# A down projection by seven products: the sums made early, in an order of their own, in place of operands that are done with

## The chip, the cores and the metric

The kernel runs on one core of a Trainium2 chip. The engines of that core are TensorE (PE in the profile, its weight loads PEld), VectorE (DVE), ScalarE (ACT), GpSimd (POOL) and SyncE (SP, which here only issues transfers). The metric is the device time of one execution in microseconds (us), lower is better. Before the change it is 1359.8 us, the median of three runs (1359.43 to 1360.07).

## The reference, cut to what matters

One layer: conditioning, two kinds of attention, an output projection, and a gated MLP with a short convolution. Only the last product of the MLP is touched here:

```python
h = modulate(rmsnorm(x, g_mlp_norm[l]), sh_m, sc_m)
u = causal_dwconv(jnp.dot(h, w_up[l]), conv_w[l], conv_b[l])
gate, val = jnp.split(u, 2, axis=-1)
x = x + g_m[:, None, :] * jnp.dot(jax.nn.silu(gate) * val, w_down[l])
```

`silu(gate) * val` is 1024 x 2816, called g below; `w_down` is 2816 x 1024. All is float32.

## The kernel before, in words

**The product.** The MLP's first half runs a loop over the 22 blocks of 128 columns of g (`for j in range(NF)`); it writes each block, transposed, to the buffer `g_d` in HBM (`store_g`). The down projection then reads g and `w_down` back. It multiplies them as 2 x 2 blocks with seven products in place of eight (a Strassen-Winograd scheme). A is g in four blocks (A11, A12, A21, A22), B is `w_down` in four (B11 to B22), and the kernel's seven products are, in the order in which it runs them (`order`, L1719):

| product | left operand | right operand |
|---|---|---|
| 1 | A11 | B11 |
| 2 | A12 | B21 |
| 7 | S3 = A11 - A21 | T3 = B22 - B12 |
| 6 | S2 = A22 - S3 | T2 = T3 + B11 |
| 5 | S1 = A21 + A22 | T1 = B12 - B11 |
| 3 | S4 = A12 - S2 | B22 |
| 4 | A22 | T4 = T2 - B21 |

**The steps.** Each product is accumulated over NK2 = 11 blocks k of 128 inner rows. `seq` lists the 77 pairs (product, k); one pair is called a step below, numbered 0 to 76: product 1 has steps 0 to 10, product 2 steps 11 to 21, product 7 steps 22 to 32, product 6 steps 33 to 43, product 5 steps 44 to 54, product 3 steps 55 to 65, product 4 steps 66 to 76. Both operands of a step are 128 x 512. For accuracy each operand is split into a rounded high part and the rest (`halves`, L1762 on: the high part by ACT, L81; the rest by DVE, L87), and a step is 4 output tiles times 3 matmuls (`mm3`, L1858 to L1860): high by high, high by low, low by high. The split operands lie in buffers `dpa` and `dpb`, five steps deep in all. Where an operand is a sum made on POOL, `halves` first copies it into PSUM by ACT (the "staged" flag, L1770, tiles `sga` and `sgb`), and DVE reads that copy.

**The sums.** `operands(i)` (L1741 on) makes a step's sums on POOL (L1744) at the point where that step's halves are written, that is, LEAD = 4 steps before TensorE's loop reaches it. The S3 sum is the one exception: it is made one product early, in product 2. Four buffers per k are kept for long: `held_a[k]` (A11, then S3, then S2), `held_b[k]` (B11) and `tsum[k]` (T3, then T2). S1, T1, S4 and T4 are written over one of the operands loaded for them.

**The loads.** Apart from the blocks of product 1, which go straight to their held buffers, every operand is loaded (`get`, `fetch`, L1704, issued by SP) into a slot of the tag "ws", of which there are ten of 128 x 512. `load_down(i)` loads what step i needs, `advance` keeps AHEAD = 4 steps beyond the one whose halves are written. Counted over all seven products there are 13 loads into slots for each k: 3 in product 2 (B21, A12, A21), 2 in product 7, 1 in product 6, 3 in product 5, 2 in product 3, 2 in product 4. There are 8 sums for each k.

**The ends of the products.** `finish_tile` empties the accumulated banks: product 2 stores its output after a multiplication by the gate row on DVE and an addition of the residual on POOL (L1834); product 6 adds on DVE and on POOL (L1829); product 5 has three DVE and three POOL operations per tile (L1837 to L1843), product 3 two on DVE and one on POOL (L1845 to L1847), product 4 two on DVE.

**What sets the order.** The program is written in the order of the loops. A scheduler that runs while the program is built then orders each engine's instructions by that order as priority and by simulated readiness, and gives tiles their slots; semaphores are added by it. On the chip each engine, and SP's queue of transfers, runs in the fixed order that results.

Of the kernel before, what the change touches and what calls it, by code (L numbers as in the profile page):

```python
# [12 lines left out]
F32 = mybir.dt.float32  # L13
# [8 lines left out]
MUL, ADD, SUB, MIN, MAX = ALU.mult, ALU.add, ALU.subtract, ALU.min, ALU.max  # L22

P = 128
# [5 lines left out]
NF = FF // P  # L30
# [17 lines left out]
PRE = 2  # L48
HI_ON, HL_BUFS = "pa", 3
VSCALE = 2.0 ** 14  # L50
UP_W = (3.2, 2.0)


# [15 lines left out]
def layer_kernel(ctx, tc, I, out):  # L69
    nc = tc.nc  # L70
    pe, act, dve, pool, sp = nc.tensor, nc.scalar, nc.vector, nc.gpsimd, nc.sync
# [412 lines left out]
    for d in range(ND):  # L484
# [25 lines left out]
        for t in range(NT):  # L510
            h, j = divmod(t, 4)
# [14 lines left out]
    def pow2_scale(nm, ssw, b2, n, fac):  # L526
# [11 lines left out]
        dve.tensor_scalar(t[:, 2, 1:2].bitcast(I32), t[:, 2, 1:2].bitcast(I32), 0x7F800000, None, op0=ALU.bitwise_and)  # L538
        dve.tensor_scalar(ab[:, 0:1], t[:, 2, 0:1], VSCALE, None, op0=MUL)
        dve.tensor_scalar(ab[:, 1:2], t[:, 2, 1:2], 1.0 / VSCALE, None, op0=MUL)  # L540
        return ab[:, 0:1], ab[:, 1:2]
# [298 lines left out]
    def f_up(gr):  # L840
        for c in f_up_steps(gr):
            yield c * UP_W[gr]

# [167 lines left out]
    def f_pre():  # L1011
        pages = [pgtile([P, 2, 2, 512], F16, f"wpp{i}") for i in range(2)]
        count = 0
        for j in range(PRE):
# [14 lines left out]
            for x in range(4):  # L1029
                pe.matmul(pt[:, 0:1], ones[:], t[:, x:x + 1], start=(x == 0), stop=(x == 3))  # L1030
            dve.tensor_scalar(t[:, 4:5], pt[:, 0:1], 1.0 / VSCALE ** 2, 1e-20, op0=MUL, op1=ADD)
            pool.tensor_tensor(t[:, 5:6], t[:, 4:5], phalf[:], op=ALU.pow)
# [310 lines left out]
    W_IN, W_M, W_UP, W_O = 21.0e3, 36.4e3, 13.0e3, 41.5e3  # L1343
    W_A = 5 * W_IN + W_M + W_UP * UP_W[0]
    W_B = W_UP * UP_W[1] + W_O
    C_CA, C_M = 6.95e3, 8.05e3
# [135 lines left out]
    def scale_ff(j, pt):  # L1482
# [5 lines left out]
        for i in range(2):  # L1488
            pe.matmul(pt[:, 0:1], ones[:], t[:, i:i + 1], start=(i == 0), stop=(i == 1))
        dve.tensor_scalar(t[:, 2:3], pt[:, 0:1], 1.0 / VSCALE ** 2, 1e-20, op0=MUL, op1=ADD)  # L1490
        pool.tensor_tensor(t[:, 3:4], t[:, 2:3], phalf[:], op=ALU.pow)
# [86 lines left out]
    def bank(tag, name, n=1):  # L1578
        return ps3.tile([P, n * 512], F32, name=name, tag=tag, bufs=1)
# [12 lines left out]
    def ff_first(j, w, held=None):  # L1592
        c = fc[j] = mt("c", [P, 7, 512], f"c{j}")
        p1 = bank("p1", f"p1_{j}")
        product(p1[:], w[0], "b11")
        act.activation(c[:, 0], p1[:], AF.Copy)
        if held:
            ff_second(j, w[1], held)
# [6 lines left out]
    def ff_tile(j):  # L1605
        held = j < 2
        w = gens.pop(j) if held else ff_w(j)
        if not held:
            ff_first(j, [next(w)])
        c = fc.pop(j)  # L1610
        p5, p6 = (bank(n, f"{n}_{j}") for n in ("p5", "p6"))
        p27, p34 = bank("p27", f"p27_{j}", 2), bank("p34", f"p34_{j}", 2)
        if not held:
            product(p27[:, :512], next(w), "b21")
        product(p27[:, 512:], next(w), "t3")
        product(p6[:], next(w), "t2")
        dve.tensor_tensor(c[:, 6], c[:, 0], p6[:], op=ADD)
        if held:
            dve.tensor_tensor(c[:, 0], c[:, 0], c[:, 5], op=ADD)
            dve.tensor_tensor(c[:, 5], c[:, 6], p27[:, 512:], op=ADD)  # L1620
        else:
            dve.tensor_tensor(c[:, 0::5][:, 0:2], c[:, 0::6][:, 0:2], p27[:].rearrange("p (a b) -> p a b", a=2), op=ADD)
        product(p5[:], next(w), "t1")
        dve.tensor_tensor(c[:, 3:5], c[:, 5:7], p5[:].unsqueeze(1).to_broadcast([P, 2, 512]), op=ADD)
        product(p34[:, 512:], next(w), "t4")
        product(p34[:, :512], next(w), "b22")
        raws.pop(j, None)
        dve.tensor_tensor(c[:, 1:3], c[:, 4:6], p34[:].rearrange("p (a b) -> p a b", a=2), op=ADD)  # L1628
        cg = c[:, 0:2].rearrange("p a b -> p (a b)")
        cv = c[:, 2:4].rearrange("p a b -> p (a b)")  # L1630
        ug, uv = conv(cg, j, 0), conv(cv, j, 1)
        act.activation(ug[:], ug[:], AF.Silu)
        dve.tensor_tensor(ug[:], ug[:], uv[:], op=MUL)
        gout.append((j, ug))
# [56 lines left out]
    NK2 = NF // 2  # L1691
    held_a, held_b, tsum = {}, {}, {}
    dpool = {}
# [20 lines left out]
    def drop(nm):  # L1714
        return mt("ws", [P, 512], nm)[:]

    plan = {1: ("A11", "B11"), 2: ("A12", "B21"), 7: ("S3", "T3"), 6: ("S2", "T2"), 5: ("S1", "T1"), 3: ("S4", "B22"),
            4: ("A22", "T4")}
    order = [1, 2, 7, 6, 5, 3, 4]  # L1719
    seq = [(p, k) for p in order for k in range(NK2)]  # L1720
    BL = {"A11": 0, "A12": 1, "A21": 2, "A22": 3, "B11": 0, "B12": 1, "B21": 2, "B22": 3}

    def get(nm, k, p):
        o = drop(f"{nm}_{p}_{k}")
        return fetch(o, (g_src if nm[0] == "A" else w_src)(BL[nm], k))

    loaded = {}

    def load_down(i):
        p, k = seq[i]  # L1730
        if p == 1:
            held_a[k], held_b[k] = hold("ha", k), hold("hb", k)
            fetch(held_b[k], w_src(0, k))
            fetch(held_a[k], g_src(0, k))
            loaded[i] = ()
        else:
            need_ = {2: ("B21", "A12", "A21"), 7: ("B22", "B12"), 6: ("A22",), 5: ("B12", "A21", "A22"), 3: ("B22", "A12"),
                     4: ("B21", "A22")}[p]
            loaded[i] = [get(nm, k, p) for nm in need_]

    def operands(i):  # L1741
        p, k = seq[i]
        x = loaded.pop(i)
        tt = lambda o, a, b, op: (pool.tensor_tensor(o, a, b, op=op), o)[1]  # L1744
        if p == 1:
            return (held_a[k], 0), (held_b[k], 0)
        if p == 2:
            tt(held_a[k], held_a[k], x[2], SUB)
            return (x[1], 0), (x[0], 0)
        if p == 7:  # L1750
            t = tsum[k] = dpool["r"].tile([P, 512], F32, name=f"tsum{k}", tag=f"tsum{k}")[:]
            return (held_a[k], 1), (tt(t, x[0], x[1], SUB), 1)
        if p == 6:
            return (tt(held_a[k], x[0], held_a[k], SUB), 1), (tt(tsum[k], tsum[k], held_b[k], ADD), 1)
        if p == 5:
            return (tt(x[1], x[1], x[2], ADD), 1), (tt(x[0], x[0], held_b[k], SUB), 1)
        if p == 3:
            return (tt(x[1], x[1], held_a[k], SUB), 1), (x[0], 0)
        return (x[1], 0), (tt(x[0], tsum[k], x[0], SUB), 1)

    def halves(i):
        p, k = seq[i]  # L1762
        pgs = []
        for nm, (src, staged) in zip("ab", operands(i)):
            pl, n = (dna, 4) if i % 5 < 2 else (dnb, 6)
            w = pl.tile([P, 2, 512], F32R, name=f"dp{nm}{p}_{k}", tag="dp", bufs=n)
            hi_of("a", w[:, 0], src)
            if staged:
                sg = ps4.tile([P, 512], F32, name=f"sg{nm}{p}_{k}", tag="sg", bufs=2)
                act.activation(sg[:], src, AF.Copy)  # L1770
                src = sg[:]
            lo_of("v", w[:, 1], src, w[:, 0])
            pgs.append(w)
        return pgs
# [3 lines left out]
    for j in range(NF):  # L1778
        if j + 3 < NF:
            load_ff(j + 3)  # L1780
        if j >= NF - 3:
            load_down(j - NF + 3)
        store_g()
        if j == NF - 1:
            ready_p += [halves(0), halves(1)]
        ff_tile(j)
        if j + 2 < NF:
            scale_ff(j + 2, bank("G", f"wss_ps{j + 2}"))
        if j >= 4:
            next(gate, None)  # L1790
# [68 lines left out]
        pe.matmul(b, g[:, 0, sl], w[:, 1], start=False, stop=False, **kw)  # L1859
        pe.matmul(b, g[:, 1, sl], w[:, 0], start=False, stop=end, **kw)  # L1860

    AHEAD = 4
    nl = [3]

    def advance(i):
        while nl[0] < min(len(seq), i + AHEAD):
            load_down(nl[0])
            nl[0] += 1

    for i, (p, k) in enumerate(seq):  # L1870
        if i == 4:
            store_g()
        while len(ready_p) + i < min(len(seq), i + LEAD):
            m = len(ready_p) + i
            advance(m)
            with tc.high_priority(offset=200) if m < 6 else nullcontext():
                ready_p.append(halves(m))
        if k == 0 and p != 2:
            for t in range(4):
                banks[t] = ps4.tile([P, 512], F32, name=f"q{p}{t}", tag="q", bufs=6)  # L1880
        tail = p == 4 and k >= NK2 - 3
        if tail and k > NK2 - 3:
            continue
        steps = ready_p[:3] if tail else ready_p[:1]
        if not tail:
            ready_p.pop(0)
        for t in range(4):
            for x, (g, w) in enumerate(steps):
                mm3(t, w, g, k == 0 and p != 2, k + x == NK2 - 1)
            if k + len(steps) == NK2:  # L1890
                finish_tile(p, t)
# [79 lines left out]
```

## Time and profile before

| | |
|---|---|
| median of three runs | 1359.8 us |
| the profiled execution's own time | 1360.98 us |
| its span, first to last instruction | 1359.2 us |
| mean granted TensorE clock | 0.969 |
| TensorE busy | 1263.4 us, 93% of the span |
| DVE, ACT, POOL busy | 75%, 64%, 56% |
| matmuls of the down projection | 924, from 1137.95 us to the end of the span |

A row of a group reads: line, engine, operation, output<-inputs by the program's names, shapes, count | busy us, mean ns of one | idle time of the engine just before them, and what ended it. In a row of the stages the count stands in brackets behind each engine's busy time, then come the granted clock, the mean busy share of the 16 transfer engines and their GB/s. Times of rows are us from the start of the span. Loads appear as `A<-g_d` and `B<-w_down` (slots) or `ha<-g_d` and `hb<-w_down` (held buffers); a sum appears with its output in place, as `ha<-ha,A` (S3), `tsum<-B,B` (T3), `ha<-A,ha` (S2), `tsum<-tsum,hb` (T2), `A<-A,A` (S1), `B<-B,hb` (T1), `A<-A,ha` (S4) and `B<-tsum,B` (T4).

### The profile page before, as it was taken

How to read it: one execution, taken by the hardware profiler on the slowest of the kernel's cores; microseconds unless marked ns; L12 is line 12 of the kernel's file. 1: busy time of each engine (PE TensorE's matmuls, PEld its weight loads, DVE VectorE, ACT ScalarE, POOL GpSimd, SP SyncE). 2: the span in 40 equal slices, each digit the busy share in tenths (PEclk: the TensorE clock that was granted, in tenths of full speed). 3: DMA queues.
4: the chain of work that ended last, by engine and by line, in shares of the span. 5: the costliest groups of instructions: out<-in, count | busy, mean ns of one | idle time of the engine just before them, and what ended most of it. 6: DMA issues, size and time to landing. Idle time of an engine off the chain costs nothing.

```text
span 1359.2 us, 20793 instructions
## 1 busy us (share of the span) xinstructions
PE 1263.4 (93%) x7016; PEld 856.7 (63%) x7016; DVE 1022.6 (75%) x1598; ACT 863.2 (64%) x1650; POOL 763.2 (56%) x888
## 2 busy tenths in 40 slices
PE   8888999999768998988997898999999999999998
PEld 7887788887545666655673344444444446888876
DVE  7848777766768876667448998988888897565677
ACT  5646666666757677775556566666666644488743
POOL 5844434243665575584100787666666661399794
PEclk6998999999989998999998999999999999999999
DMA  9412333331111044444354432222222025584763
GB/s 346 142 50 66 117 96 99 104 104 46 38 43 32 17 131 146 144 155 136 128 213 163 170 97 103 88 89 74 93 78 94 32 92 203 191 291 148 268 221 129
DMA packets 102758, 169.07 MB, mean 124 GB/s; under 512 B 10742, under 2 KB 50938, under 8 KB 102652
## 3 DMA queue, kind: packets, MB, share of 16 engines
q1 hardware_dynamic: 102652, 167.75, 36.9%
q8 instruction: 55, 0.90, 0.3%
q14 instruction: 51, 0.42, 0.1%
HBM read 135.20 MB, written 32.51 MB: 123 GB/s over the span
## 4 chain that ended last, share of the span: by engine, by line
PE 61%; DVE 15%; ACT 6%; issue 6%; POOL 6%; DMA 5%; SPq 0%; DVEq 0%; POOLq 0%; ACTq 0%
PE p L1514 7%; PE p L1513 7%; PE p L1515 7%; PE q L1859 3%; PE q L1860 3%; PE q L1858 3%; PE tm L1212 2%; PE tc L1212 2%; DVE mz L1169 1%; DVE adaw L505 1%; PE ipq L212 1%; PE ipq L213 1%; PE ipq L214 1%; PE ipv L212 1%; PE ipv L213 1%
## 5 line engine op out<-in xcount | busy, mean ns | idle before, releaser
L1859 PE MATMUL q<-dpb,dpa 128*128 128x512 f32 x308 | 120.5, 391 | 3.5 <-DVE dpb L87 3.5
L1858 PE MATMUL q<-dpb,dpa 128*128 128x512 f32 x308 | 120.3, 392 | 1.4 <-ACT dpb L81 0.8
L1860 PE MATMUL q<-dpb,dpa 128*128 128x512 f32 x308 | 118.7, 389 | 0.0
L1223 DVE TENSOR_TENSOR hlm<-pm,hlm 128x512 f16<-128x512 f32 (+3 forms) x96 | 69.6, 733 | 39.9 <-POOL hlm L83 22.1
L1585 ACT ACTIVATE u<-c,pk,wcv 128x1024 f32<-128x1024 f32 x44 | 52.1, 1232 | 39.3 <-DVE c L1628 35.0
L1586 DVE SCALAR_TENSOR_TENSOR u<-c,wcv,u 128x1023 f32<-128x1023 f32 x44 | 56.9, 1329 | 25.8 <-ACT u L1585 25.8
L1212 PE MATMUL tm<-qt,kt 96*128 96x512 f16 (+7 forms) x288 | 68.9, 331 | 4.6 <-ACT qt L1178 3.0
L1216 ACT ACTIVATE pm<-tm,scm 128x512 f32<-128x512 f32 (+1 forms) x96 | 55.2, 579 | 28.2 <-PE tm L1212 21.2
L1223 DVE TENSOR_TENSOR hlc<-pc,hlc 128x256 f16<-128x256 f32 (+3 forms) x96 | 53.9, 570 | 23.7 <-POOL hlc L83 15.7
L1216 ACT ACTIVATE pc<-tc,sca 128x512 f32<-128x512 f32 (+3 forms) x96 | 49.9, 525 | 31.7 <-DVE hlc L1223 15.7
L83 POOL TENSOR_SCALAR hlm<-pm 128x384 f16<-128x384 f32 (+2 forms) x48 | 27.3, 568 | 74.8 <-ACT pm L1216 45.2
L1859 PEld LDWEIGHTS q<-dpb,dpa 128*128 128x128 f32 x308 | 57.8, 188 | 17.0 <-DVE dpb L87 5.1
L1858 PEld LDWEIGHTS q<-dpb,dpa 128*128 128x128 f32 x308 | 57.8, 188 | 15.1 <-DVE xo L1845 1.3
L1860 PEld LDWEIGHTS q<-dpb,dpa 128*128 128x128 f32 x308 | 57.8, 188 | 11.9
L1212 PEld LDWEIGHTS <-kt 128*128 128x128 f16 (+2 forms) x480 | 45.5, 100 | 29.1 <-issue 11.2
L81 ACT ACTIVATE wd<-wu 128x512 f16<-128x512 f32 x20 | 12.6, 629 | 80.2 <-DVE wu L1525 80.2
L87 DVE TENSOR_TENSOR dpa<-sga,dpa 128x512 fp32r<-128x512 f32 x44 | 30.2, 689 | 42.9 <-ACT dpa L81 29.2
L1506 POOL TENSOR_TENSOR wa<-wu,wa 128x512 f16<-128x512 f32 x20 | 33.8, 1688 | 48.1 <-ACT wa L81 47.9
L212 PE MATMUL ipq<-wq_s,hT 128*128 128x256 f32 x192 | 58.8, 306 | 0.0
L1212 PE MATMUL tc<-qt,kt 128*128 128x512 f16 (+3 forms) x192 | 53.6, 309 | 5.5 <-ACT pc L1216 2.6
L1587 DVE SCALAR_TENSOR_TENSOR u<-c,wcv,u 128x1022 f32<-128x1022 f32 x44 | 58.3, 1354 | 0.0
L214 PE MATMUL ipq<-wq_s,hT 128*128 128x256 f32 x192 | 57.8, 301 | 0.0
(546 smaller groups left out, 4763.6 us busy)
## 6 DMA issues: line engine op xcount, KB each, us to landing
wu<-w_up SPq DMA_DIRECT2D x40, 512.0 KB, 4.1
A<-g_d SPq DMA_DIRECT2D x77, 256.0 KB, 3.7
B<-w_down SPq DMA_DIRECT2D x66, 256.0 KB, 4.4
aw<-w_ada SPq DMA_DIRECT2D x96, 128.0 KB, 2.1
g_d<-u SPq DMA_DIRECT2D x22, 512.0 KB, 2.6
adaw<-w_ada_a SPq DMA_DIRECT2D x16, 512.0 KB, 6.0
x<-x SPq DMA_DIRECT2D x8, 512.0 KB, 9.3
wq_r<-w_qk SPq DMA_DIRECT2D x32, 128.0 KB, 2.3
```

Source lines behind the costliest of these rows:

```text
L212: pe.matmul(pt, sh, mh, start=(start and i == 0), stop=False)
L214: pe.matmul(pt, sl, mh, start=False, stop=(stop and i == n - 1))
L1212: last = pe.matmul(s[:, c0:c1], l, m, start=(y == 0), stop=(y == len(todo) - 1))
L1216: recent["a"] = act.activation(p[:, :w], s[:, :w], AF.Exp, scale=ninv)
L1223: lo = recent["v"] = dve.tensor_tensor(hl[:, 1, :w], p[:, :w], hl[:, 0, :w], op=SUB)
L1513: pe.matmul(pt, sh, pg[:, 0], start=(k == 0), stop=False)
L1514: pe.matmul(pt, sh, pg[:, 1], start=False, stop=False)
L1515: pe.matmul(pt, sl, pg[:, 0], start=False, stop=(k == 3))
L1587: dve.scalar_tensor_tensor(u[:, 2:], c[:, :S - 2], sv[:, 0:1], u[:, 2:], op0=MUL, op1=ADD)
L1858: pe.matmul(b, g[:, 0, sl], w[:, 0], start=first, stop=False, **kw)
L1859: pe.matmul(b, g[:, 0, sl], w[:, 1], start=False, stop=False, **kw)
L1860: pe.matmul(b, g[:, 1, sl], w[:, 0], start=False, stop=end, **kw)
```

## The change

The sums get a schedule apart from the steps that use them. A list of jobs holds, for each step m, the step's own halves ("H", m), and behind it the sums that are given to m: for block k, S3 behind step 3 + k, T3 behind 11 + k, S2 and T2 behind 22 + k, T1 behind 33 + k, S4 behind 34 + k, S1 behind 41 + k and T4 behind 47 + k. Loads are issued job by job, up to JAHEAD = 9 jobs ahead and as long as no more than ten slots are taken; a sum's operands are loaded for the sum, a plain operand for its step. S4 is now written over `held_a[k]`, T1 over `held_b[k]`, T4 over `tsum[k]`; S1 stays in the slot of one of its operands until its step. T4 is no longer staged through PSUM. There are again 13 loads into slots and 8 sums for each k.

```diff
+JAHEAD = 9
...
-    def load_down(i):
-        p, k = seq[i]
-        if p == 1:
+    loaded, s1 = {}, {}
+    sums = {}
+    for k in range(NK2):
+        for nm, m in (("S3", 3), ("T3", 11), ("S2", 22), ("T2", 22), ("T1", 33), ("S4", 34), ("S1", 41), ("T4", 47)):
+            sums.setdefault(m + k, []).append((nm, k))
+    jobs = []
+    for m in range(len(seq)):
+        jobs += [("H", m)] + sums.get(m, [])
+    need_of = {"S3": ("A21",), "T3": ("B22", "B12"), "S2": ("A22",), "T2": (), "T1": ("B12",), "S4": ("A12",),
+               "S1": ("A21", "A22"), "T4": ("B21",), 2: ("B21", "A12"), 7: (), 6: (), 5: (), 3: ("B22",), 4: ("A22",)}
+    busy = [0]
+
+    def load_job(x):
+        nm, k = x
+        if nm == "H":
+            nm, k = seq[k]
+        if nm == 1:
             held_a[k], held_b[k] = hold("ha", k), hold("hb", k)
             fetch(held_b[k], w_src(0, k))
             fetch(held_a[k], g_src(0, k))
-            loaded[i] = ()
+            return True
+        names = need_of[nm]
+        if busy[0] + len(names) > 10:
+            return False
+        busy[0] += len(names)
+        loaded[nm, k] = [get(a, k, nm) for a in names]
+        return True
+
+    def make_sum(nm, k):
+        x = loaded.pop((nm, k))
+        busy[0] -= len(x) - (nm == "S1")
+        tt = lambda o, a, b, op: pool.tensor_tensor(o, a, b, op=op)
+        if nm == "S3":
+            tt(held_a[k], held_a[k], x[0], SUB)
+        elif nm == "T3":
+            t = tsum[k] = dpool["r"].tile([P, 512], F32, name=f"tsum{k}", tag=f"tsum{k}")[:]
+            tt(t, x[0], x[1], SUB)
+        elif nm in ("S2", "S4"):
+            tt(held_a[k], x[0], held_a[k], SUB)
+        elif nm == "T2":
+            tt(tsum[k], tsum[k], held_b[k], ADD)
+        elif nm == "T1":
+            tt(held_b[k], x[0], held_b[k], SUB)
+        elif nm == "S1":
+            tt(x[1], x[0], x[1], ADD)
+            s1[k] = x[1]
         else:
-            need_ = {2: ("B21", "A12", "A21"), 7: ("B22", "B12"), 6: ("A22",), 5: ("B12", "A21", "A22"), 3: ("B22", "A12"),
-                     4: ("B21", "A22")}[p]
-            loaded[i] = [get(nm, k, p) for nm in need_]
+            tt(tsum[k], tsum[k], x[0], SUB)
 
     def operands(i):
         p, k = seq[i]
-        x = loaded.pop(i)
-        tt = lambda o, a, b, op: (pool.tensor_tensor(o, a, b, op=op), o)[1]
+        x = loaded.pop((p, k), ())
+        busy[0] -= len(x) + (p == 5)
         if p == 1:
             return (held_a[k], 0), (held_b[k], 0)
         if p == 2:
-            tt(held_a[k], held_a[k], x[2], SUB)
             return (x[1], 0), (x[0], 0)
-        if p == 7:
-            t = tsum[k] = dpool["r"].tile([P, 512], F32, name=f"tsum{k}", tag=f"tsum{k}")[:]
-            return (held_a[k], 1), (tt(t, x[0], x[1], SUB), 1)
-        if p == 6:
-            return (tt(held_a[k], x[0], held_a[k], SUB), 1), (tt(tsum[k], tsum[k], held_b[k], ADD), 1)
+        if p in (7, 6):
+            return (held_a[k], 1), (tsum[k], 1)
         if p == 5:
-            return (tt(x[1], x[1], x[2], ADD), 1), (tt(x[0], x[0], held_b[k], SUB), 1)
+            return (s1[k], 1), (held_b[k], 1)
         if p == 3:
-            return (tt(x[1], x[1], held_a[k], SUB), 1), (x[0], 0)
-        return (x[1], 0), (tt(x[0], tsum[k], x[0], SUB), 1)
+            return (held_a[k], 1), (x[0], 0)
+        return (x[0], 0), (tsum[k], 0)
...
         if j >= NF - 3:
-            load_down(j - NF + 3)
+            assert load_job(jobs[j - NF + 3])
         store_g()
         if j == NF - 1:
             ready_p += [halves(0), halves(1)]
+            at_job = 2
...
-    def advance(i):
-        while nl[0] < min(len(seq), i + AHEAD):
-            load_down(nl[0])
+    def advance(a):
+        while nl[0] < len(jobs) and nl[0] < a + JAHEAD and load_job(jobs[nl[0]]):
             nl[0] += 1
+        assert nl[0] > a
...
             m = len(ready_p) + i
-            advance(m)
+            while True:
+                advance(at_job)
+                nm, x = jobs[at_job]
+                at_job += 1
+                if nm == "H":
+                    break
+                make_sum(nm, x)
```

More of the change, by code (lines that the diff above doesn't have):

```diff
@@ L1715, in drop @@
         return mt("ws", [P, 512], nm)[:]
-    plan = {1: ("A11", "B11"), 2: ("A12", "B21"), 7: ("S3", "T3"), 6: ("S2", "T2"), 5: ("S1", "T1"), 3: ("S4", "B22"),
-            4: ("A22", "T4")}
     order = [1, 2, 7, 6, 5, 3, 4]
@@ L1725, in get @@
         return fetch(o, (g_src if nm[0] == "A" else w_src)(BL[nm], k))
-    loaded = {}
-    def load_down(i):
-        p, k = seq[i]
-        if p == 1:
+    loaded, s1 = {}, {}
[14 more added lines that the diff above has]
+        if nm == 1:
             held_a[k], held_b[k] = hold("ha", k), hold("hb", k)
@@ L1860, in mm3 @@
         pe.matmul(b, g[:, 1, sl], w[:, 0], start=False, stop=end, **kw)
-    AHEAD = 4
     nl = [3]
-    def advance(i):
-        while nl[0] < min(len(seq), i + AHEAD):
-            load_down(nl[0])
+    def advance(a):
+        while nl[0] < len(jobs) and nl[0] < a + JAHEAD and load_job(jobs[nl[0]]):
             nl[0] += 1
+        assert nl[0] > a
     for i, (p, k) in enumerate(seq):
```

## The prediction, made before the changed kernel ran

> **What bounds the kernel now.** I read the page's head first, then the busy time by stages, the chain of waits (its first and last matmul of the down projection), and who waited for whom.
>
> ```profile
> span 1359.2 us, 20793 instructions
> ```
>
> ```profile
> 1113.00:1137.00 24.00, 24.00 (x113) 10.97 (x112) 19.92 (x20) 9.35 (x14) 7.74 (x7) 1.00 0.93 324
> 1137.95:1301.06 163.11, 163.11 (x720) 134.90 (x720) 102.19 (x138) 112.67 (x202) 112.39 (x86) 1.00 0.59 199
> 1142.00:1158.00 16.00, 16.00 (x72) 13.27 (x71) 12.43 (x17) 7.92 (x14) 0.19 (x1) 1.00 0.13 49
> 1158.00:1180.00 22.00, 22.00 (x98) 18.20 (x97) 12.59 (x17) 11.45 (x21) 7.00 (x5) 1.00 0.52 173
> 1180.00:1195.00 15.00, 15.00 (x68) 12.40 (x67) 7.65 (x10) 6.28 (x13) 9.22 (x7) 1.00 0.88 285
> 1211.00:1246.00 35.00, 35.00 (x157) 28.96 (x156) 17.85 (x28) 30.84 (x59) 35.00 (x29) 1.00 0.46 153
> 1301.06:1338.19 37.13, 32.30 (x136) 24.76 (x134) 28.55 (x32) 16.52 (x31) 35.08 (x23) 1.00 0.76 252
> 1338.19:1354.47 16.28, 16.27 (x71) 12.87 (x69) 10.94 (x16) 6.37 (x12) 3.56 (x3) 1.00 0.22 82
> ```
>
> ```profile
> 1137.95 0.23 PE q L1858
> ...
> 1354.23 0.24 PE q L1860
> ```
>
> The change touches only the down projection. In the chain it starts on TensorE at 1137.95 and ends there at 1354.47, after 216.5 us. Up to 1301.06 TensorE never stops: 720 matmuls in 163.11 us, 0.2265 us each, at a granted clock of 1.00; a step of 12 matmuls takes 2.72 us. From 1301.06 to 1338.19 only 136 are done; at the same pace they need 30.8 us, so this stretch loses 37.13 - 30.8 = **6.3 us**. The rest runs at pace again (71 x 0.2265 = 16.1 of 16.28). All that a better order of POOL's work can win is in that one stretch, the end of product 3 and most of product 4. The stops are these, for TensorE and then for ACT, which feeds it:
>
> ```profile
> PE q L1859 <- DVE dpb L87: 3.5, 3, 1.4
> PE q L1858 <- ACT dpb L81: 0.8, 1, 0.8
> PE q L1858 <- DVE xo L1845: 0.5, 1, 0.5
> ```
>
> ```profile
> ACT sgb L1770 <- DVE dpb L87: 9.2, 3, 5.3
> ACT dpa L81 <- POOL A L1744: 7.7, 1, 7.7
> ACT sgb L1770 <- POOL B L1744: 2.8, 2, 1.7
> ```
>
> They add to 4.8 us; the other 1.5 us is the slow restart behind each. The halves were late, and ACT stood 7.7 us for one sum of POOL (S4) and 2.8 us for T4. POOL was full, 35.08 of 37.13 us, with this (groups from 1301 to 1340):
>
> ```profile
> L1744 POOL TENSOR_TENSOR B<-tsum,B 128x512 f32<-128x512 f32 x11 | 17.1, 1567 | 2.1 <-DMA B<-w_down 2.0
> L1847 POOL TENSOR_TENSOR xo<-xo,x1r 128x512 f32<-128x512 f32 x4 | 7.0, 1759 | 0.0
> L1840 POOL TENSOR_TENSOR xo<-xo,x1r 128x512 f32<-128x512 f32 x3 | 4.8, 1616 | 0.0
> L1843 POOL TENSOR_TENSOR u<-u,x1r 128x512 f32<-128x512 f32 x3 | 4.8, 1587 | 0.0
> L1842 POOL TENSOR_TENSOR u<-u,gmbc 128x512 f32<-128x512 f32 x2 | 3.4, 1739 | 0.0
> L1744 POOL TENSOR_TENSOR A<-A,ha 128x512 f32<-128x512 f32 x2 | 2.5, 1282 | 0.0
> ```
>
> Of the 25 operations 13 are sums (19.6 us), queued among product 5's and 3's output work, which cannot run earlier.
>
> **The change, part by part.**
>
> *Sums out of products 3 and 4.* The last sum, T4 of k = 10, is now placed behind step 57. Its halves are written some four steps ahead of TensorE, so POOL is done with sums about when product 5 ends (step 55 begins at 1137.95 + 55 x 2.72 = 1287.6). The 19.6 us above leave the stretch; POOL keeps at most the other 20.0 us, and no step of products 3 and 4 waits for POOL. Worth: the 6.3 us, all of it if nothing else is late next. Next in line is DVE, 28.55 of 37.13 us busy there.
>
> *T4 unstaged.* Eleven ACT copies go (L1770, 0.6 us each in the first row below); ACT is only 16.52 of 37.13 us busy, so nothing. DVE then reads that operand from SBUF. Rows of the same kind from 1320 to 1347, product 4:
>
> ```profile
> L1770 ACT ACTIVATE sgb<-B 128x512 f32<-128x512 f32 x9 | 5.4, 597 | 12.9 <-DVE dpb L87 11.2 <-POOL B L1744 1.7
> L87 DVE TENSOR_TENSOR dpa<-A,dpa 128x512 fp32r<-128x512 f32 x9 | 10.5, 1163 | 5.0 <-ACT dpa L81 5.0
> L87 DVE TENSOR_TENSOR dpb<-sgb,dpb 128x512 fp32r<-128x512 f32 x10 | 6.8, 680 | 0.0
> L1846 DVE TENSOR_TENSOR xo<-xo,gmbc 128x512 f32<-128x512 f32 x4 | 4.8, 1229 | 0.0
> L1845 DVE TENSOR_TENSOR xo<-u,q 128x512 f32<-128x512 f32 x4 | 2.6, 674 | 0.0
> ```
>
> Unstaged costs 0.68 at best and 1.16 us at the mean beside a full POOL. Bounds for 22 such operations: 22 x 0.68 = 15.0 to 22 x 1.163 = 25.6 us; with product 3's eight output operations (4.8 + 2.6 = 7.4 us) 22.4 to 33.0 us against 11 steps of 2.72 = 29.9. Even the high end is 3.1 us over, less than the four steps of lead (10.9 us); and POOL now has four operations there (7.0 us) in place of fifteen. I take 0 to 1 us, 0. What weighs against it is a rule of the Trainium skill, "SBUF — State Buffer", section "Who interferes with whom": a VectorE instruction with two SBUF inputs and a GpSimd instruction that reads SBUF exclude each other. The trace agrees (1163 against 680 ns); by the rule the price falls with POOL's work, so it does not move the sum.
>
> *Sums earlier: is POOL able to?* The pace of sums without contention:
>
> ```profile
> 1216.80 7.57 POOL L1744 TENSOR_TENSOR ha<-A,ha 128x512 f32<-128x512 f32 x6
> ```
>
> That is 1.26 us each, 29 in 35 us in the stage 1211 to 1246. S3 and T3 (22 sums) move into products 1 and 2, where POOL is nearly idle (0.19 of 16 us, 7.00 of 22). The crowded stretch is from step 22's halves to the last S1. S2 of a block may overwrite its operand only when step 22 + k has been split; the split buffers are five deep, so from 1137.95 + 18 x 2.72 = 1186.9 on. S1 of k = 10 must be there for step 54 (1284.8) less some 3.1 us for four ACT operations and one of DVE: 1281.7. In those 94.8 us POOL does S2, T2, T1, S4 and S1 (55), five T4, and 8 output operations of products 2 and 6: 68 x 1.26 = 85.7 us. It fits, with 9.1 us to spare; cost 0. The spare is what its waits may eat. They were, from 1190 to the end:
>
> ```profile
> POOL A L1744 <- DVE xo L1839: 5.3, 1, 5.3
> POOL A L1744 <- DMA A<-g_d: 3.9, 5, 1.3
> POOL B L1744 <- DMA B<-w_down: 3.7, 3, 2.0
> POOL tsum L1744 <- ACT dpb L81: 2.0, 1, 2.0
> POOL tsum L1744 <- DMA B<-w_down: 1.8, 2, 1.4
> ```
>
> Without the first (output work of product 5) 11.4 us, so at that price POOL would be 2.3 us late. The new waits, of S2 and T2 for ACT, stand eleven steps before their sums are used; queued behind them on POOL are only sums with more slack. I take 0, with 2.3 us as the other end (and up to one step more, below). Nothing is gained there, since TensorE had no stop before 1301.
>
> *The loads.* As many as before, 13 per k, on the same SP queue; but T3's 22 move from product 7 up into product 2. Up to the halves of step 21 SP must now bring 22 + 22 + 11 (S3) + 20 (T3) = 75 blocks of 0.262 MB. Before, of these or their like came, by 1137:
>
> ```profile
> hb<-w_down SPq DMA_DIRECT2D x8, 256.0 KB, 5.1
> ha<-g_d SPq DMA_DIRECT2D x8, 256.0 KB, 5.3
> A<-g_d SPq DMA_DIRECT2D x7, 256.0 KB, 5.8
> B<-w_down SPq DMA_DIRECT2D x4, 256.0 KB, 5.9
> ```
>
> 27, and six of the 22 earlier: 33. Left are 42, from 1137 to 1192.0 (step 21 at 1195.1 less 3.1): 55 us, 1.31 us each, 200 GB/s. The rates by stages above are 324, 49, 173, 285 GB/s. The 49 is no limit of the engines: the ten slots were full with product 2's blocks, which wait for their step.
>
> ```profile
> 1142.21 0.32 SPq L1704 DMA_DIRECT2D A<-g_d  x1
> 1158.49 0.32 SPq L1704 DMA_DIRECT2D A<-g_d  x1
> ```
>
> Now the slots hold S3's and T3's operands at that time, which POOL clears by itself, so loads can flow there. Even if these 16 us stay empty, 42 loads in 39 us need 282 GB/s, what the stage 1180 to 1195 had. I take 0; below nothing is excluded, because TensorE lost nothing here; the other end is under the rivals.
>
> **Sum.** -6.3 for the stops, +0.1 left over at restarts: **-6.2 us**. The profiled execution took 1360.98 us in all (1.78 around its span); it would be 1354.8. The median is 1.2 lower: 1359.8 - 6.2 = **1353.6 us**.
>
> **The rivals.**
>
> *POOL late in product 5.* Its waits eat the spare: 2.3 us late, and up to a step of 2.7 us more where POOL's fixed order puts product 6's additions, which wait for TensorE, ahead of an S1. That gives 1353.6 + 5.0 = 1358.6. For it: POOL without a gap from 1211 to 1246 already now. Against: then its sums were due within four steps, now most have eleven.
>
> *The slots starve product 2* (slower). If the ten slots, not the transfer engines, set the rate, as between 1142 and 1180, product 2's halves come late and TensorE stops at about steps 14 to 21, before anything is won. From an empty stretch to 1158 on, at the mean rate of the down projection, 199 GB/s, a block takes 1.32 us: 16 + 42 x 1.32 = 71.3 us, 16.3 late, and 1353.6 + 16.3 = 1369.9. It decides below (16 + 42 x 0.262/r = 55 + 8.9) 230 GB/s; at 173 it would be 1378. For it: four blocks per step in place of three. Against: the two rates of 285 and 324 beside it.
>
> *It does not do what it says.* The scheduler puts sums where it sees room: six S2 stand in a row in the line above, though the program has T2 between them. If its order ends up as late as now, 1359.8.
>
> **Chances.** Forecast 0.55, POOL late 0.15, slots 0.20, no effect 0.10. A measurement of this kernel tells 0.2%, 2.7 us, from no change. Faster: 0.55 and a third of the second case, 0.60; same: the rest of it and the last, 0.20; slower 0.20. Range: 1352.6 (all 6.3 us, the 0.2 us after 1338, and 0.7 for spread) to 1364.0, which leaves out two thirds of the slot case (0.13) and some 0.04 below. The likeliest case's own range is 1352.6 to 1355.0.
>
> **What would show it.** Right: TensorE's idle time in 1301 to 1338 falls from 4.8 us to under 1; POOL's last sum ends before 1295; ACT waits for no POOL sum in products 3 and 4; POOL's gap between 1142 and 1158 fills; DVE's unstaged operations in product 4 near 0.7 us. Wrong: a wait of TensorE before 1301, with loads behind it in product 2 or S1 (A<-A,A) in product 5; or the stops of products 3 and 4 still there with POOL idle, which would make DVE their cause.

## The result, and the profile after

| | median us | runs | lowest to highest | ratio to before, 95% interval |
|---|---|---|---|---|
| before | 1359.93 | 4 | 1359.43 to 1363.31 | |
| after | 1372.36 | 4 | 1371.01 to 1376.59 | 1.0082 [1.0058, 1.0105] |

The kernel became slower by 0.8% (0.0082 x 1359.9 = 11.2 us), where 6.2 us less had been forecast. The profiled execution of after took 1376.59 us. Lines are shifted by the diff: L82 is the high part on ACT, L88 the rest on DVE, L1757 the sums, L1800 the staging copies, L1889 to L1891 the matmuls. Operands loaded for a sum are now called `A_S` and `B_T`.

```profile
span 1374.8 us, 20765 instructions
```

This execution begins its down projection at 1143.29 us, before's at 1137.38 (the 1137.95 given ahead is where the chain of waits enters it, 0.57 us later; the last matmul of before ends at 1354.46, 4.7 us ahead of the end of the span). Ten profiles of kernels with one or another order of the sums begin it between these two times, and one with the same code as after up to product 4 begins it at 1137.92, so this shift of 5.9 us is scatter between executions. What counts is the length, from the start of the first matmul to that of the last: 216.7 us before, **226.6 us after**. The 924 matmuls at the pace of 0.2265 us need 209.3, so the loss inside the down projection grew from 7.4 to 17.3 us, by 9.9.

The busy time by stages shows where. The columns are those of the prediction's stages; the loss is the length less the number of matmuls times 0.2265 us. A matmul that straddles a border is counted on both sides, so each loss reads up to 0.4 us too small.

```profile
1143.29:1160.00 16.71, 15.68 (x68) 12.48 (x67) 11.61 (x13) 8.89 (x14) 7.71 (x3) 1.00 0.50 185
1160.00:1180.00 20.00, 20.00 (x90) 16.55 (x89) 16.54 (x17) 10.38 (x19) 11.55 (x7) 1.00 0.64 209
1180.00:1195.00 15.00, 15.00 (x68) 12.43 (x67) 4.11 (x7) 4.35 (x8) 6.48 (x4) 1.00 0.75 257
1195.00:1211.00 16.00, 14.47 (x56) 11.21 (x55) 7.08 (x12) 8.38 (x16) 8.57 (x7) 0.89 0.92 298
1211.00:1250.00 39.00, 38.52 (x169) 31.25 (x168) 22.17 (x35) 35.66 (x67) 35.01 (x29) 1.00 0.47 168
1250.00:1292.80 42.80, 40.43 (x176) 32.36 (x175) 18.81 (x30) 26.75 (x50) 42.80 (x35) 1.00 0.69 229
1292.80:1325.63 32.83, 28.60 (x114) 21.72 (x113) 29.58 (x32) 18.99 (x35) 26.21 (x20) 0.95 0.71 233
1325.63:1369.86 44.23, 44.23 (x197) 36.60 (x195) 30.56 (x44) 15.78 (x28) 9.49 (x6) 1.00 0.31 106
```

From 1325.63 on, the later half of product 3 and all of product 4, nothing is lost: there the change did what it says. The loss sits at four places that had none before, or less: 1.3 us at the start, 16.00 - 56 x 0.2265 = 3.3 us at the end of product 2, 42.80 - 176 x 0.2265 = 2.9 us in product 5, and 32.83 - 114 x 0.2265 = 7.0 us across the end of product 5 and the first half of product 3. Whom TensorE waited for in the down projection, total, times and longest:

```profile
PE q L1890 <- DVE dpb L88: 4.6, 4, 3.8
PE q L1889 <- DVE u L1859: 1.7, 1, 1.7
PE q L1889 <- ACT dpb L82: 1.5, 2, 1.2
PE q L1889 <- DVE c L1629: 1.0, 1, 1.0
PE q L1889 <- DVE xo L1864: 0.5, 1, 0.5
```

These add to 9.3 us of 17.3. The rest is slow restarts, and half clock, told at the end.

*End of product 2 (step 20).* The timeline of POOL (start, duration, operation, idle before and what ended it):

```profile
1197.55 1.28 POOL L1757 TENSOR_TENSOR tsum<-B_T,B_T 128x512 f32<-128x512 f32 x1 [4.33 <-DMA B_T<-w_down]
1201.75 1.29 POOL L1757 TENSOR_TENSOR tsum<-B_T,B_T 128x512 f32<-128x512 f32 x1 [2.91 <-DMA B_T<-w_down]
1205.00 1.28 POOL L1757 TENSOR_TENSOR tsum<-B_T,B_T 128x512 f32<-128x512 f32 x1 [1.97 <-DMA B_T<-w_down]
1206.24 1.29 POOL L1757 TENSOR_TENSOR ha<-A_S,ha 128x512 f32<-128x512 f32 x1
```

And the timeline of ACT at the same time, which writes the halves of product 2:

```profile
1186.15 0.63 ACT L82 ACTIVATE dpa<-A 128x512 fp32r<-128x512 f32 x1 [2.31 <-DMA A<-g_d]
...
1190.11 0.63 ACT L82 ACTIVATE dpa<-A 128x512 fp32r<-128x512 f32 x1 [2.81 <-DMA A<-g_d]
```

Both stand waiting for loads, a step each 4.0 us where TensorE takes 2.72. The lead of four steps is eaten up at step 20. The loads in turn waited for slots. For whom SP's queue waited from 1143 to 1201 us (total, times, longest):

```profile
SPq L1705 <- POOL tsum L1757: 19.5, 9, 3.6
SPq L1705 <- POOL ha L1757: 14.3, 5, 10.0
```

So SP stood 33.8 of 58 us until a T3 sum (`tsum`) or an S3 sum (`ha`) of POOL had cleared a slot, while POOL's T3 sums waited for loads. POOL, which is idle meanwhile, gets to its first S2 (`ha<-A_S,ha`) only at 1206.24, because in its fixed order that sum stands behind the last T3.

*End of product 5 and start of product 3.* One timeline view, POOL, DVE and TensorE:

```profile
1295.37 7.54 POOL L1757 TENSOR_TENSOR tsum<-tsum,B_T 128x512 f32<-128x512 f32 x6
...
1298.71 4.74 DVE L88 TENSOR_TENSOR dpb<-B,dpb 128x512 fp32r<-128x512 f32 x1 [0.39 <-ACT dpb L82]
...
1315.63 5.15 DVE L1870 TENSOR_TENSOR xo<-xo,gmbc 128x512 f32<-128x512 f32 x3
...
1322.51 0.80 PE L1890 MATMUL q<-dpb,dpa 128*128 128x512 f32 x1 [3.75 <-DVE dpb L88]
```

One DVE operation, the rest of product 3's B22 with both inputs in SBUF, took 4.74 us beside a run of six T4 sums without a gap, which ended at 1302.91; it ended 0.54 us behind them. DVE then does product 5's output work in arrears; three of these operations, beside POOL's own, take 5.15 us where 0.68 each is the least seen. Step 60 finds its halves missing from 1318.8 on.

### The profile page after: what moved, and what is told of

It is laid out like the page before. It is cut to its first block, busy times and chain, and to the rows that moved or that the text cites. A ratio compares the mean times of both kernels' runs of the same rounds, so it can differ in the third digit from the quotient of the medians.

```text
span 1374.8 us, 20765 instructions
## 1 busy us (share of the span) xinstructions
PE 1274.4 (93%) x7016; PEld 860.2 (63%) x7016; DVE 1023.8 (74%) x1598; ACT 857.3 (62%) x1639; POOL 767.3 (56%) x888
## 4 chain that ended last, share of the span: by engine, by line
PE 58%; DVE 16%; POOL 8%; ACT 7%; issue 6%; DMA 5%; SPq 1%; DVEq 0%; POOLq 0%; ACTq 0%
PE p L1515 7%; PE p L1514 7%; PE p L1516 7%; PE q L1890 3%; PE q L1889 3%; PE q L1891 3%; PE tc L1213 2%; PE tm L1213 2%; PE ipq L213 1%; PE ipq L214 1%; PE ipq L215 1%; DVE adaw L506 1%; DVE mz L1170 1%; DMA wq_r<-w_qk 1%; PE ipv L213 1%
## 5 line engine op out<-in xcount | busy, mean ns | idle before, releaser
L1889 PE MATMUL q<-dpb,dpa 128*128 128x512 f32 x308 | 122.1, 397 | 4.8 <-DVE u L1859 1.7
L1890 PE MATMUL q<-dpb,dpa 128*128 128x512 f32 x308 | 121.8, 396 | 4.7 <-DVE dpb L88 4.6
L1891 PE MATMUL q<-dpb,dpa 128*128 128x512 f32 x308 | 120.1, 394 | 0.1
L1889 PEld LDWEIGHTS q<-dpb,dpa 128*128 128x128 f32 x308 | 58.5, 190 | 20.6 <-DVE u L1859 2.5
L1217 ACT ACTIVATE pc<-tc,sca 128x512 f32<-128x512 f32 (+3 forms) x96 | 49.9, 525 | 30.7 <-PE tc L1213 14.6
L1891 PEld LDWEIGHTS q<-dpb,dpa 128*128 128x128 f32 x308 | 58.6, 190 | 12.6 <-DVE dpa L88 0.4
L88 DVE TENSOR_TENSOR dpa<-sga,dpa 128x512 fp32r<-128x512 f32 x44 | 30.2, 689 | 44.6 <-ACT dpa L82 30.7
L82 ACT ACTIVATE wd<-wu 128x512 f16<-128x512 f32 x20 | 12.6, 629 | 80.1 <-DVE wu L1526 80.1
L1507 POOL TENSOR_TENSOR wa<-wu,wa 128x512 f16<-128x512 f32 x20 | 33.8, 1689 | 48.1 <-ACT wa L82 47.9
```

The source lines that it names most:

```text
L1217: recent["a"] = act.activation(p[:, :w], s[:, :w], AF.Exp, scale=ninv)
L1889: pe.matmul(b, g[:, 0, sl], w[:, 0], start=first, stop=False, **kw)
```

## The experiments

All kernels below compute the whole result; each edit is against after. "Length" is again that of the down projection in the profiled execution, one execution each, while the ratios come from many runs; the two agree within about 4.5 us, so a length shows where, and the ratio how much. The kernel before, run beside them, had a median of 1363.71 us with the first four and 1364.38 with the last four.

**T3 ahead of S3.** T3's loads move to product 1, S3's to product 2.

```diff
-("S3", 3), ("T3", 11), ("S2", 22)
+("S3", 11), ("T3", 2), ("S2", 22)
```

> S3 goes back to 11 + k, T3 to 2 + k, in product 1, where its two loads wait for nothing but a slot; all else as in the change. Theory (product 2 asks four blocks a step of ten slots; its halves and T3 come late, and every later sum on POOL with them): no stop of TensorE in products 2 and 5, the last T3 sum ended before 1180 us, ratio to before 0.994 to 0.999. Rival 1 (POOL is too full from step 22 to 54 whatever comes before): the stop in product 5 stays at 3 to 4 us, ratio 1.000 to 1.004. Rival 2 (the sums among the last tile of the first half cost the time): only the 1.3 us at the start go, ratio about 1.007.

1363.06 us, ratio 0.999 [0.9969, 1.001], length 218.2. T3 by its durations (least, median, most) and its first and last start, then TensorE's waits and DVE's slow operation:

```profile
L1757 POOL TENSOR_TENSOR tsum<-B_T,B_T x11: 1287/1737/5160, 1130.6 to 1169.3; 128x512 f32<-128x512 f32 x11
```

```profile
PE q L1890 <- DVE dpb L88: 3.7, 1, 3.7
PE q L1889 <- ACT u L1852: 2.1, 1, 2.1
```

```profile
1285.63 4.74 DVE L88 TENSOR_TENSOR dpb<-B,dpb 128x512 fp32r<-128x512 f32 x1 [0.39 <-ACT dpb L82]
```

With T3 out of product 2 the stops at the end of product 2 and in product 5 are both gone, the second though no sum of product 5 was moved: the delay of POOL's sums in product 2 was carried on through POOL's order (more on this under the last experiment). The ratio is at the upper end of what was expected, because two stops are left, one at step 11 where ACT's emptying of product 1's banks now stands behind a load, and the one at step 60, with its 4.74 us operation.

**Fourteen slots.** The order stays; T3's operands get four slots of their own.

```diff
-o = drop(f"{nm}_{p}_{k}")
+o = drop(f"{nm}_{p}_{k}") if p != "T3" else dpool["r"].tile([P, 512], F32, name=f"{nm}_{p}_{k}", tag="xs", bufs=4)[:]
...
-if busy[0] + len(names) > 10:
+c = nm == "T3"
+if busy[c] + len(names) > (10, 4)[c]:
```

> The change with four slots more, which T3's operands use alone; order of sums unchanged. Theory, if the slots set the rate in product 2: its late halves and the gaps between T3 sums go, the stop near step 20 goes, the product 5 stop shrinks; ratio 0.998 to 1.003. Rival (the transfer engines set the rate, four blocks a step are 385 GB/s): the same stop near step 20, ratio 1.007 to 1.010, with 290 GB/s or more in the stage.

1363.58 us, ratio 0.9964 [0.9941, 0.9987], length 216.35. The stages, T3, and TensorE's waits:

```profile
1160.00:1180.00 20.00, 18.90 (x83) 15.02 (x82) 18.55 (x16) 11.43 (x21) 14.08 (x9) 1.00 0.84 265
1180.00:1195.00 15.00, 15.00 (x68) 12.42 (x67) 8.30 (x10) 5.77 (x10) 6.74 (x5) 1.00 0.91 316
```

```profile
L1758 POOL TENSOR_TENSOR tsum<-B_T,B_T x11: 1282/1297/1745, 1158.5 to 1193.4; 128x512 f32<-128x512 f32 x11
```

```profile
PE q L1891 <- DVE dpb L88: 3.4, 3, 2.3
PE q L1890 <- DVE c L1629: 2.1, 1, 2.1
```

The same loads, some of the first ones in another order (the scheduler moved them), flow at 265 and 316 GB/s where ten slots gave 209 and 257 (its down projection begins only 1.4 us earlier, so the stages compare). SP's waits for T3 sums fall to

```profile
SPq L1705 <- POOL tsum L1758: 10.3, 9, 2.1
```

T3 is done at 1194.7 in place of 1206.3, and the stops at step 20 and in product 5 go. Stops of 0.85 and 0.24 us at step 11, the first of product 2, are new. The transfer engines were not the limit; the slots were, and 10.2 us of length hung on them (226.6 - 216.35). Split by products, the loss falls by 2.1 us in product 2, 1.1 in product 7, 3.5 in product 5 and 4.6 in product 3, and grows by 1.1 in product 1. So the start and step 60 stay, but of the 7.0 us around step 60 more than half hung on the slots too: DVE came to that place later, and the longer stop brought half clock. The ratio is better than the 0.998 to 1.003 expected.

**T3 in product 7.** Behind the steps 21 + k, nearly where it was before the change.

```diff
-("T3", 11)
+("T3", 21)
```

> T3 back in front of its own step (21 + k), so that product 2 loads three blocks a step at most; S2, T2 and the rest stay where the change has them. Theory: no stop in product 2, but POOL now has three sums a step in product 7, 79 operations of 1.26 us = 99.5 us in 94.8 us before the last S1, so the stops in products 5 and 3 stay or grow: ratio 1.003 to 1.010. If POOL's load in products 7 to 5 did not matter, 0.996 to 1.000.

1370.91 us, ratio 1.0045 [1.002, 1.007], length 223.6. Product 2 is free of stops, but ACT now waits for sums from 1210 to 1245:

```profile
ACT dpb L82 <- POOL tsum L1757: 10.2, 4, 4.8
```

TensorE stops 1.41 and 1.82 us at steps 31 and 32, then at steps 54 and 60. With T3 in the crowded stretch POOL is too slow, as the working of its pace had it: eleven sums more are 13.9 us, and the spare was 9.1. These stops in product 7 were not expected; the stop expected to stay or grow in product 3 became smaller (1.12 us). So T3 has to come ahead of product 7: in product 2 with more slots, or in product 1 as in the first experiment.

**T4 staged again.**

```diff
-return (x[0], 0), (tsum[k], 0)
+return (x[0], 0), (tsum[k], 1)
```

> The change with T4 copied into PSUM by ACT again before DVE reads it. Theory: product 4 has no stop in the changed kernel, so nothing changes, ratio 1.007 to 1.010. Rival (DVE operations with two SBUF inputs beside POOL cost the time in product 4): ratio 1.001 to 1.006.

1374.47 us, ratio 1.0079 [1.0049, 1.0109], length 229.1. Not distinguishable from after: the unstaged T4 is not what costs.

**Fourteen slots, and product 3's B22 staged.** As above, and the operand of the 4.74 us operation goes through PSUM.

```diff
-return (held_a[k], 1), (x[0], 0)
+return (held_a[k], 1), (x[0], 1)
```

> The kernel with 14 slots, and B22 of product 3 is copied into PSUM by ACT before DVE reads it (one copy of 0.6 us a step more on ACT). Theory (the stop at step 60 begins where a DVE operation with two SBUF inputs stood 4.75 us behind six T4 sums that ran on POOL without a gap): that operation takes 0.7 us, TensorE's stop of 2.3 us at step 60 goes, ratio 0.2% below the 14-slot kernel's 0.9964. Rival (the twelve output operations of product 5 on DVE are the cause, whatever stands before them): the stop stays at 2 us or more.

1358.43 us, ratio 0.9965 [0.9949, 0.998], length 213.6. POOL's run of T4 is still there, and DVE beside it in the same timeline:

```profile
1280.02 7.56 POOL L1758 TENSOR_TENSOR tsum<-tsum,B_T 128x512 f32<-128x512 f32 x6
...
1284.45 0.68 DVE L88 TENSOR_TENSOR dpb<-sgb,dpb 128x512 fp32r<-128x512 f32 x1
...
1286.53 0.68 DVE L88 TENSOR_TENSOR dpb<-sgb,dpb 128x512 fp32r<-128x512 f32 x1
```

These are the first two B22 operations of product 3. With one input in PSUM the same operation takes 0.68 us beside the same run, and step 60 does not stop. This shows the cause of that stop; product 5's output operations alone, the rival, don't make it. What it is worth only the length tells (2.7 us, one execution each); the ratio is that of the fourteen slots alone, where 0.2% less was expected.

**Fourteen slots, and T4 spread over every second step** (behind 47 + 2k).

```diff
-("T4", 47)
+("T4", 47 + k)
```

> The kernel with 14 slots, and T4 of block k behind step 47 + 2k in place of 47 + k, so that T4's last sums fall among product 5's output work in product 3 and not in one run before it. Theory: no DVE operation of more than 2 us around step 55, the stop at step 60 goes or is under 1 us; POOL stays busy to 1315 and nothing waits for it; ratio 0.993 to 0.997. Rival (POOL's work in product 3 is what stopped the kernel before the change, and it comes back): stops in steps 62 to 70, ratio 0.997 to 1.001.

1360.42 us, ratio 0.9982 [0.9965, 0.9998], length 214.5. The stop at step 60 shrinks from 2.35 to 0.74 us: breaking up the run helps as staging does, and the exclusion between POOL and DVE is again the cause. The ratio is not better than that of the fourteen slots alone, and worse than the 0.993 to 0.997 expected.

**All together, S3 later.** Fourteen slots, B22 staged, S3 behind 11 + k and T3 behind 5 + k, so that no extra load goes into the tail of the first half.

```diff
-("S3", 3), ("T3", 11), ("S2", 22)
+("S3", 11), ("T3", 5), ("S2", 22)
```

> 14 slots, B22 staged, S3 behind 11 + k (out of the last tile of the first half) and T3 behind 5 + k. Theory: the stop of 2.1 us at the start goes too, and none takes its place: no stop over 0.5 us in the down projection, ratio 0.990 to 0.995. Rival (T3 sums in product 1 exclude DVE's unstaged halves there, and ACT's copies of product 1's banks stand behind a late load): a stop of 1 to 3 us near step 11, ratio 0.995 to 0.999.

1358.47 us, ratio 0.9959 [0.9941, 0.9977], length 212.8, the shortest. The stop at the start is gone, but two stops are left where none over 0.5 us was expected:

```profile
PE q L1891 <- DVE dpb L88: 1.6, 1, 1.6
PE q L1890 <- DVE u L1860: 0.9, 1, 0.9
```

It beats the kernel before by 0.4% (0.0041 x 1364.4 = 5.6 us), less than the 0.990 to 0.995 expected; by its ratio it can't be told from the kernel with fourteen slots alone (0.9964).

**Only S3 later,** at the ten slots.

```diff
-("S3", 3)
+("S3", 11)
```

> The change with S3 behind 11 + k again and nothing else; product 2 then loads five blocks a step into ten slots. Theory: the stop at the start goes (1 to 2 us), the stops of product 2 and after it grow: ratio 1.008 to 1.016. Rival (S3 in product 1 and the last tile costs most of the time): ratio 1.000 to 1.006.

1371.69 us, ratio 1.0061 [1.0037, 1.0084], length 228.5. The start's stop goes, and product 2 gets worse, with S3's loads back among its own:

```profile
1195.00:1211.00 16.00, 13.01 (x40) 9.37 (x41) 8.97 (x10) 7.36 (x14) 13.26 (x10) 0.79 1.00 343
```

Here 16.00 - 40 x 0.2265 = 6.9 us are lost, against 3.3 in after. The direction was as expected, the total lower than the 1.008 to 1.016 of the slot theory; the interval reaches that range and the rival's (to 1.006) alike, so the total does not decide, and the stops do.

Product 5 has no stop in this run, although product 2 is late. The traces show what goes with a stop there: how far POOL's first S1 sum begins ahead of TensorE's step 44, the first of product 5. It is 10.4 us in after, 10.5 with T4 staged and 12.9 with all together, and these three have a stop at step 45. It is 14.6 us in this last kernel and 14.5 to 19.5 in the other six, which have none at steps 44 to 46.

## Why the prediction was wrong, step by step

*Sums out of products 3 and 4: the mechanism held.* ACT, which stood 7.7 and 2.8 us for sums of POOL, waits for none from 1297 us on, and TensorE stops nowhere from 1325.63 on. The promised 6.3 us were there to be had (the kernel with fourteen slots and B22 staged loses nothing in products 3 and 4), and after gave back more than that earlier.

*The loads, "I take 0": the first step that failed.* The prediction compared 200 GB/s needed with 285 and 324 seen, and concluded that loads would flow because POOL clears the slots of the sums' operands by itself. It did not:

```profile
1151.26 5.21 POOL L1757 TENSOR_TENSOR ha<-ha,A_S 128x512 f32<-128x512 f32 x1 [10.06 <-DVE dpa L88]
```

An S3 sum overwrites `held_a[k]`, which DVE must have split for product 1 first; the prediction asked for this in S2 and not in S3. So the sums stood, the slots stayed full, and SP issued no operand from 1145.82 to 1156.50. That is the case for which the prediction itself asked 282 GB/s afterwards. With four blocks a step in product 2 the ten slots gave 209 and 257 GB/s, and a step came every 4.0 us. The last block for step 21 was there at 1203.06, when ACT's wait for it ended, 59.8 us after the start in place of 55. A slot is held from the issue of its load until its step or sum has used it, and a load into it can't be issued earlier; the fourteen-slot kernel, whose text differs in nothing else, shows that this was the bound: it has the same early wait (9.4 us for an S3 sum) and makes it up. The rival "The slots starve product 2" had the cause right. Its price was too high, 16.3 us: the stops in product 2 cost 3.7 us, the 3.3 of the stage and what its borders count twice. Its time, 1369.9, comes near the measured 1372.36 in part by luck: in length after lies 16.1 us above the forecast's 210.5, and of these 10.2 hang on the slots over all products, 2.7 on B22 of product 3, and the rest on the start and step 11.

*Sums earlier, "It fits, with 9.1 us to spare": failed with it.* The working of POOL's pace was right (it was busy 35.01 of 39.00 us in the stage 1211 to 1250 and all of the 42.80 in the next, and T3 in product 7 overloads it). Its starting point was not. S2 was to begin at 1186.9; it began at 1206.24, which less the shift of 5.9 is 1200.3, or 13.4 us late, and the last S1 ended at 1289.5 by the same clock, 7.8 us late. With fourteen slots (shift 4.5) S2 began at 1192.5, and the last S1 ended at 1280.7, 1.0 us ahead of the 1281.7 allowed: there it fits. The prediction reckoned that S2 is allowed from step 18 on, and overlooked that in POOL's fixed order it comes behind T3, which waits for loads. POOL then ran behind until product 5, where ACT waits for S1:

```profile
ACT sga L1800 <- POOL A_S L1757: 10.1, 5, 2.8
ACT dpa L82 <- POOL A_S L1757: 5.0, 4, 2.9
```

TensorE's stop of 1.7 us there is at one remove: DVE has the halves of product 5 ahead of emptying product 6's banks (`u`, L1859), these halves wait through ACT for an S1 sum, and TensorE needs the bank. That is the rival "POOL late in product 5", 2.9 us in its stage against 5.0 priced, but on top of the other and not in place of it. The two were weighed as alternatives; in after they are one chain, since the fourteen slots remove both. They are not bound to come together: the last two experiments have one without the other.

*"POOL is done with sums about when product 5 ends", "Next in line is DVE": named, and not priced.* The last T4 ended at 1302.9, in before's time 1297.0, where under 1295 was said. The price of an unstaged DVE operation was taken as 0.68 to 1.163 us, and only for product 4. There it was right:

```profile
L88 DVE TENSOR_TENSOR dpb<-tsum,dpb 128x512 fp32r<-128x512 f32 x11 | 9.7, 882 | 0.0
L88 DVE TENSOR_TENSOR dpa<-A,dpa 128x512 fp32r<-128x512 f32 x11 | 8.6, 786 | 4.6 <-ACT dpa L82 4.6
```

But product 3's B22, which was unstaged all along, now meets the T4 sums. Before, its eleven operations took 1.777 us at most:

```profile
L87 DVE TENSOR_TENSOR dpb<-B,dpb x11: 677/1180/1777, 1279.2 to 1314.9; 128x512 fp32r<-128x512 f32 x11
```

One of 4.74 us, at the moment when DVE also has product 5's output to do, is what the upper bound missed. The two kernels that remove it (staged, or T4 spread) remove all or most of the stop at step 60. The rule that the prediction weighed, of the Trainium skill, "SBUF — State Buffer", section "Who interferes with whom", was the right one to weigh, and its conclusion "the price falls with POOL's work" was drawn for product 4 alone.

*The start: not foreseen at all.* S3 behind step 3 puts loads into the last tiles of the first half. The chain of waits there:

```profile
1132.40 0.38 SPq L1705
...
1132.88 4.94 DMA hb<-w_down
...
1137.85 0.64 ACT dpb L82
...
1141.75 1.14 DVE c L1623
...
1144.31 1.23 DVE c L1629
...
1145.59 0.49 PE q L1889
```

In SP's order `hb`, an operand of product 1, is issued late, at 1132.40; ACT and DVE split it first and so come late to the last tile's additions (L1618 to L1629), which TensorE waits for. It cost 1.3 us; the kernels with S3 behind 11 + k do not have this stop.

*"No effect" and the loss before 1301 as a sign of error.* The sign named (a wait of TensorE before 1301 with loads behind it in product 2, or S1 in product 5) is what came, both parts of it.

What stays open: the 1.6 us left in the kernel with all together, the stops at step 11 that came with fourteen slots, and what in POOL's order brought S1 early enough in the last run. The 0.9 us of the former is again a bank of product 6, with the first S1 only 12.9 us ahead.

## What to carry to other kernels

A buffer pool is a rate: slots times block size over the time that a slot is held. Before loads are moved into a stage, compare that rate with the stage's demand, not the bandwidth that another stage reached. Here ten slots at four blocks per 2.72 us leave 6.8 us for each block in its slot, and fourteen leave 9.5. Of this the transfer alone took some 4 us (256 KB each, median from issue to landing, 1160 to 1200 us in after):

```profile
B_T<-w_down SPq DMA_DIRECT2D x17, 256.0 KB, 4.2
```

The 4.0 us a step that were measured are 10 us a block in ten slots. A sum that may run early runs only when everything ahead of it in its engine's fixed order has run, so a late load moves all of them. And where a sum is moved to, look for two-input operations on the other engine there, also those that the change doesn't touch.

## What the hardware showed that was not expected

**DVE can stand behind a whole run of POOL.** An operation of 0.68 us took 4.74 or 4.75 us in five kernels, beside a run of six POOL sums at a pitch of 1.26 us, of which it met the last four. The excess, 4.06 us, is over three POOL instructions. With T3 in product 7 it met all six, and stood longer still:

```profile
L88 DVE TENSOR_TENSOR dpb<-B,dpb x1: 6800/6800/6800, 1293.8 to 1293.8; 128x512 fp32r<-128x512 f32 x1
```

In all six kernels it ended some 0.55 us behind the last sum of the run, whatever the point at which it had begun. The Trainium skill ("SBUF — State Buffer", "Who interferes with whom") says that the two contend there, and of VectorE's two-port modes that whoever issues first holds the shared ports for the whole instruction; a wait for one instruction would be 1.26 us here, and the measured ones are longer. In before, and in `xo<-xo,gmbc` above (5.15 us for three), the engines took turns. What decides between the two was not found.

**A stop costs more than its length.** At the end of step 60's stop the granted clock fell to half:

```profile
1322.51:1325.63 3.12, 3.12 (x7) 2.49 (x8) 3.12 (x3) 1.67 (x3) 3.12 (x3) 0.51 0.77 267
```

Seven matmuls at 0.426 us in place of 0.2265 are 1.4 us more on a stop of 3.75. The same came at the end of product 2, though no single stop there was over 1.3 us:

```profile
1199.23:1202.27 3.04, 1.51 (x6) 0.71 (x5) 1.29 (x2) 1.15 (x2) 0.52 (x1) 1.00 0.90 309
1202.68:1206.08 3.40, 3.40 (x10) 2.61 (x9) 2.36 (x4) 2.63 (x5) 1.44 (x2) 0.50 0.96 311
```

Here a stretch with six matmuls in 3.04 us, half idle, went ahead of the fall; a stop of 2.35 us in the fourteen-slot kernel brought none. The Trainium skill ("TensorE: Matmul & The Clock Gate", "What's actually happening") gives two states, half and full, a window of about 3.4 us, and half clock after an idle window. The trace agrees on 0.50 and on 3.40 us; but the stretch before this fall was not idle throughout. How much idle time it takes was not found.
